# Opening of a transformer-block kernel: running sum of squares moved from GpSimd to VectorE, and two tiles of v ahead of the sums

## The chip, the cores and the metric

One Trainium2 chip, one of its cores. The metric is the device time of one execution in microseconds (us); lower is better. Times of a kernel are medians over several executions. In the text PE is TensorE (matrix multiply), DVE is VectorE, ACT is ScalarE, POOL is GpSimd, SP is the engine that only issues transfers here.

## The reference, cut to what matters

The kernel computes one residual block over L = 1040 positions (16 meta tokens and 1024 frames) of width 1024, in float32. What the change touches is the first normalisation and the projections that follow it:

```python
def _rmsnorm(x, w):
    x32 = x.astype(jnp.float32)
    y = x32 * lax.rsqrt(jnp.mean(x32 * x32, axis=-1, keepdims=True) + EPS)
    return (y * w.astype(jnp.float32)).astype(x.dtype)
...
    n1 = _rmsnorm(h, norm1_w)
    proj = n1 @ w_in.astype(h.dtype)
    q, k, v, fg, u = jnp.split(
        proj, [D_ATTN, 2 * D_ATTN, 3 * D_ATTN, 3 * D_ATTN + N_HEADS], axis=-1)
    q = _rmsnorm(q.reshape(B, L, N_HEADS, HEAD_DIM), q_norm_w).transpose(0, 2, 1, 3)
    k = _rmsnorm(k.reshape(B, L, N_HEADS, HEAD_DIM), k_norm_w).transpose(0, 2, 1, 3)
```

Forgetting attention over 8 heads, pooling heads, an output projection and a SwiGLU feed-forward part come after it and are not touched.

## The kernel before, in words

**Layout.** The input arrives transposed, as hT: 8 tiles (`KT`) of 128 rows of the width by 1040 positions. Since the factor rsqrt(mean) belongs to a position, it can be multiplied in after the projection; the projections therefore start on x times the norm's weight while the sums of squares are still being made.

**Split products.** Each matrix product runs as three products of rounded operands: high by high, low by high, high by low. A tile is split by ACT writing the rounded high part (`xh`, L187; `wh`, L157 and L125) and DVE writing the rest (`xl`, L188; `wl`, L160 and L128). For the weights of v DVE also writes the last 384 columns of the high part (L159).

**The opening loop (L175 to L218), one pass for each of the 8 row tiles k.** SP loads xs (L179, L181). ACT writes xh (L187), DVE writes xl (L188). ACT squares xs into a tile of its own (L197 for k = 0, which is the accumulator `sqacc`, L200 for the others), and POOL adds that tile to `sqacc` (L201). PE multiplies: the first pair of heads of k (`k0_ps`, 3 PSUM banks) and the forget gate (`fg_ps`, 3 banks) take 9 matmuls that need xh alone (L205 to L207) and then 6 that need xl (L209, L210), 15 in all for each k. At k = 3 seven small loads are issued from ACT's queue (L213, L216). At k = 6 and 7 `prep_v` loads and splits the first two of the four weight pairs of v; the other two follow behind the loop (L223). The raw weights pass through three staging buffers (`aux`), which they share with the weight `wk0s` and the later projections, so the fourth raw pair is loaded into the buffer of the first, once DVE's split of the first (L160) is done.

**Behind the loop.** ACT takes the gate's sums out of PSUM (L227). `v_mm(j)` makes the tile of v for 128 positions, 24 matmuls of 512 columns into one bank (L240 to L242), and `v_evac(j)` takes it out, scaled by the norm's factor (L247), which is why it must wait for that factor. Before the change `v_mm(0)` comes first; then `sqacc` is split (L125 by ACT, L128 by DVE), PE sums it over the partitions, once into a column form (`pc`, 18 small matmuls, L258, L259) and once into a row form (three banks, L271, L272), and DVE and ACT make the factor `rcol` from `pc` (L264 to L268) and the row `qrow` (L273). Then come `v_mm(1)`, the normalisation of the first heads of k (`qk_evac`, matmuls L287, L288), and the loop of the other seven tiles of v (L378), into which the steps of the generator `gates()` (L318) are placed at j = 2, 4, 6 and 8.

**What sets the order.** The kernel runs under a manual schedule: each engine's instructions stand in the order in which the code writes them, and an instruction waits in it for whatever made its inputs and for the last reader of a buffer that it overwrites. PSUM has 8 banks here, handed out in the order in which they came free (`PSP`, L50). ACT, SP and POOL each have one queue, in program order, for computing and for issuing transfers alike.

```python
            sq = ut(L, FT, "sq")
            A.activation(sq, xs, AF.Square)
            G.tensor_tensor(sqacc, sqacc, sq, op=OP.add)
```

Of the kernel before, what the change touches and what calls it, by code (L numbers as in the profile page):

```python
# [7 lines left out]
FT = mybir.dt.float32  # L8
FR = mybir.dt.float32r
AF = mybir.ActivationFunctionType  # L10
OP = mybir.AluOpType
# [3 lines left out]
KT = D // 128  # L15
META = 16
SEQ = 1024
L = META + SEQ
# [5 lines left out]
ST = 9  # L24
# [3 lines left out]
CHQ = ((16, 512), (528, 512))  # L28
PRE = 1
VC, VK = 640, 6  # L30
RA, LW = 10, 4
NB = (3, 6)
CW, KW, SW, W1 = 2, 2, 3, 3
# [12 lines left out]
def block_kernel(ctx, tc, hT, n1w, w_f, w_v, w_u, w_qk, b_f, qnw, knw, w_pool, pscale, w_out, n2w, w_g, w_up, w_d, outT):  # L46
# [8 lines left out]
    def nm(s):  # L55
        cnt[0] += 1
        return f"{s}_{cnt[0]}"

    def ut(cols, dt=FT, s="u"):
        return U.tile([128, cols], dt, tag="u", bufs=NU, padded_shape=None, name=nm(s))  # L60
# [4 lines left out]
    def ps(s="ps"):  # L65
        return PSP.tile([128, 512], FT, tag="ps", name=nm(s))

    def const(shape, dt, s):
        return U.tile(shape, dt, name=s, bufs=1)

    def f(ap):
        return ap.bitcast(FT)

    mm = nc.tensor.matmul
    V, A, G = nc.vector, nc.scalar, nc.gpsimd

    def table(i):

        A.add_instruction(mybir.InstLoadActFuncSet(name=nc.get_next_instruction_name(), engine=mybir.EngineType.Activation,
                                                   act_func_set_id=i, ins=[], outs=[]))  # L80
# [41 lines left out]
    def split_w(stage, cols, mk, he, le):  # L122
        h, l = mk(cols, FR, "wh"), mk(cols, FR, "wl")
        if he is A:
            A.activation(h, stage, AF.Copy)  # L125
        else:
            he.tensor_copy(h, stage)
        le.tensor_tensor(l, stage, f(h), op=OP.subtract)  # L128
        return h, l

    def load(src, cols, mk, eng=None):
        t = mk(cols, FT, "wst")
        (eng or nc.sync).dma_start(t, src)
        return t
# [4 lines left out]
    def rsqrt_newton(g, t, tmp, e1=None):  # L139

        (e1 or V).tensor_tensor(tmp, t, g, op=OP.mult)
        V.scalar_tensor_tensor(tmp, tmp, -0.5, g, op0=OP.mult, op1=OP.mult)
        V.scalar_tensor_tensor(g, tmp, 1.5, g, op0=OP.add, op1=OP.mult)


    table(6)
    xh, xl = [], []
    sqacc = None
    wfs = const([128, KT, 16], FR, "wfs")
    fg_ps = [ps("fg") for _ in CH3]  # L150
    k0_ps = [ps("k0") for _ in CH3]
# [2 lines left out]
    def prep_v(i):  # L154
        s = load(w_v[:, 2 * i:2 * i + 2, :].rearrange("p k f -> p (k f)"), 1024, aux)
        h, l = ut(1024, FR, "wh"), ut(1024, FR, "wl")
        A.activation(h[:, :VC], s[:, :VC], AF.Copy)  # L157
        if VC < 1024:
            V.tensor_copy(h[:, VC:], s[:, VC:])  # L159
        V.tensor_tensor(l, s, f(h), op=OP.subtract)  # L160
        wv.append((h, l))
# [5 lines left out]
    def wk0_split(W):  # L167
        A.activation(wk0h[:, W], wk0s[:, W], AF.Copy)
        V.tensor_tensor(wk0l[:, W], wk0s[:, W], f(wk0h)[:, W], op=OP.subtract)
# [5 lines left out]
    for k in range(KT):  # L175
        xs = ut(L, FT, "xs")
        if k == 0:
            for o, n in CH3:
                nc.sync.dma_start(xs[:, o:o + n], hT[:, 0, o:o + n])  # L179
        else:  # L180
            nc.sync.dma_start(xs, hT[:, k, :])  # L181
        if k == 0:
            wk0_split(slice(0, 128))
            wf3 = wf.rearrange("p (k f) -> p k f", k=KT)
        h, l = ut(L, FR, "xh"), ut(L, FR, "xl")
        for o, n in CH3 if k == 0 else [(0, L)]:
            A.activation(h[:, o:o + n], xs[:, o:o + n], AF.Copy, scale=n1[:, k:k + 1])  # L187
            V.scalar_tensor_tensor(l[:, o:o + n], xs[:, o:o + n], n1[:, k:k + 1], f(h)[:, o:o + n], op0=OP.mult, op1=OP.subtract)  # L188
            if k == 0 and o == 0:
                V.tensor_copy(wfs[:, :, 0:8], wf3)  # L190
                V.tensor_tensor(wfs[:, :, 8:16], wf3, f(wfs)[:, :, 0:8], op=OP.subtract)
        xh.append(h)
        xl.append(l)
        if k == 0:
            wk0_split(slice(128, 1024))
            sqacc = ut(L, FT, "sqacc")
            A.activation(sqacc, xs, AF.Square)  # L197
        else:
            sq = ut(L, FT, "sq")
            A.activation(sq, xs, AF.Square)  # L200
            G.tensor_tensor(sqacc, sqacc, sq, op=OP.add)  # L201
        s0, s1 = k == 0, k == KT - 1
        W = slice(128 * k, 128 * k + 128)
        for c, (o, n) in enumerate(CH3):
            mm(k0_ps[c][:, :n], wk0h[:, W], h[:, o:o + n], start=s0, stop=False)  # L205
            mm(k0_ps[c][:, :n], wk0l[:, W], h[:, o:o + n], start=False, stop=False)
            mm(fg_ps[c][:16, :n], wfs[:, k, :], h[:, o:o + n], start=s0, stop=False)  # L207
        for c, (o, n) in enumerate(CH3):
            mm(k0_ps[c][:, :n], wk0h[:, W], l[:, o:o + n], start=False, stop=s1)  # L209
            mm(fg_ps[c][:16, :n], wfs[:, k, :], l[:, o:o + n], start=False, stop=s1)  # L210
        if k == 3:
            for t, src in ((n2, n2w), (psc, pscale), (bfg, bass.AP(tensor=b_f.tensor, offset=b_f.offset, ap=[[0, 128], [1, NH]]))):
                A.dma_start(t, src)  # L213
            for t, src in ((qw, qnw), (kw, knw)):
                for i in range(2):
                    A.dma_start(t[64 * i:64 * i + 64], src)  # L216
        if k >= VK:
            prep_v(k - VK)  # L218
# [3 lines left out]

    for i in range(KT - VK, 4):  # L223
        prep_v(i)
    fgT = ut(L, FT, "fgT")
    for c, (o, n) in enumerate(CH3):
        A.activation(fgT[:16, o:o + n], fg_ps[c][:16, :n], AF.Copy)  # L227
# [5 lines left out]
    def v_mm(j):  # L233
        sz = min(128, L - 128 * j)
        T = slice(128 * j, 128 * j + sz)
        p = ps("v")
        for k in range(KT):
            vh, vl = wv[k // 2]
            W = slice(512 * (k % 2), 512 * (k % 2) + 512)
            mm(p[:sz], xh[k][:, T], vh[:, W], start=k == 0, stop=False)  # L240
            mm(p[:sz], xh[k][:, T], vl[:, W], start=False, stop=False)  # L241
            mm(p[:sz], xl[k][:, T], vh[:, W], start=False, stop=k == KT - 1)  # L242
        return p

    def v_evac(j, p):
        sz = min(128, L - 128 * j)
        A.activation(v32[j // 2][:sz, 512 * (j % 2):512 * (j % 2) + 512], p[:sz], AF.Copy, scale=rcol[:sz, j:j + 1])  # L247

    vp = v_mm(0)


    acch, accl = split_w(sqacc, L, ut, A, V)
# [26 lines left out]
    def qk_evac(p, n, cols, w, out):  # L279
        h, l, s = hs(n, FR, "sqh"), hs(n, FR, "sql"), hs(n, FT, "sq")  # L280
        A.activation(h, p[:, :n], AF.Square)
        A.activation(s, p[:, :n], AF.Square)
        V.tensor_tensor(l, s, f(h), op=OP.subtract)

        def rest():
            p2 = ps("ss")
            mm(p2[:, :n], bones, h, start=True, stop=False)  # L287
            mm(p2[:, :n], bones, l, start=False, stop=True)  # L288
            t, g, s2 = hs(n, FT, "t"), hs(n, FT, "g"), hs(n, FT, "s2")
            V.scalar_tensor_tensor(t, qrow[:, cols], 64.0 * EPS, p2[:, :n], op0=OP.mult, op1=OP.add)  # L290
            A.activation(g, t, AF.Ln)
            A.activation(g, g, AF.Exp, scale=-0.5)  # L292
            G.tensor_tensor(s2, t, g, op=OP.mult)  # L293

            def last():
                V.scalar_tensor_tensor(s2, s2, -0.5, g, op0=OP.mult, op1=OP.mult)
                V.scalar_tensor_tensor(g, s2, 1.5, g, op0=OP.add, op1=OP.mult)
                V.scalar_tensor_tensor(out, p[:, :n], w, g, op0=OP.mult, op1=OP.mult)
            later.append(last)
        later.append(rest)  # L300
# [5 lines left out]
    k32[0] = ut(L, FT, "k32")  # L306
    for (o, n), p in zip(CH3, k0_ps):
        qk_evac(p, n, slice(o, o + n), kw, k32[0][:, o:o + n])
    vn = v_mm(1)
    v_evac(0, vp)  # L310
    vp = vn
    now, later[:] = later[:], []
    run_later(now)
# [59 lines left out]
    def load_w(x):  # L373
        c, i = order[x]
        return load((w_u[i] if c == "u" else w_qk[2 * i + (c == "k")]).rearrange("p k f -> p (k f)"), 1024, aux)

    gt = gates()
    for j in range(2, ST):  # L378
        vn = v_mm(j)
        v_evac(j - 1, vp)  # L380
        vp = vn
        if j % 2 == 0:
            next(gt, None)
        if j == 2:
            A.activation(rb, qrow, AF.Ln)
            A.activation(rb, rb, AF.Exp, scale=-0.5)
            rtm = ut(L, FT, "rtm")
            rsqrt_newton(rb, qrow, rtm)
        if j == 6:
            staged.append(load_w(0))  # L390
        if j == 7:
            staged.append(load_w(1))
            wcur = split_w(staged.pop(0), 1024, ut, A, V)
# [1050 lines left out]
```

## Time and profile before

| | |
|---|---|
| median of 3 executions | 1170.41 us (1169.87 to 1171.07) |
| the profiled execution, its own time | 1168.22 us |
| its span in the profile | 1166.4 us |
| its mean granted clock of PE | 0.99 |
| PE busy | 1122.6 us (96%) |
| DVE busy | 764.6 us (66%) |
| ACT busy | 487.1 us (42%) |
| POOL busy | 405.7 us (35%) |

All rows below come from the one profiled execution; its own time is 1.8 us over its span and 2.2 us under the median. Times in rows are microseconds from the start of the span. In a timeline a row gives the start, the length, the engine, the line of the kernel, the operation, what it writes <- what it reads with shapes, the count of merged instructions, and in brackets how long the engine had been idle and what ended that. The length of a merged row runs from the first start to the last end. Engines with a q (ACTq, SPq) are the queues that issue transfers. A PE row's length includes its drain, which overlaps the next matmul, so PE's pace is read from the differences of starts. A granted clock of 1.00 is 2.4 GHz, 0.50 is 1.2 GHz; a value between is a mean over both.

### The profile page before, as it was taken

To read this page: it belongs to the slowest core of one execution; us is meant where nothing else is said; L and a number is where in the kernel's file an instruction comes from. 1 tells how busy PE (TensorE), PEld (TensorE's weight loads), DVE (VectorE), ACT (ScalarE), POOL (GpSimd) and SP (SyncE) were. 2 spreads that over 40 slices of the span, in tenths; PEclk is the share of its full clock that TensorE was granted. 3 is DMA by queue.
4 is the path that set the end of the run, shared out by engine and by line. 5 is a ranking of instruction groups with operands and counts; after the bars stand their busy time and mean duration, and the time that the engine had idled before them with its cause. 6 is when DMAs were issued, how large, how long until landed. Compare 5 with 4: busy or idle time off the path is not lost.

```text
span 1166.4 us, 14589 instructions
## 1 busy us (share of the span) xinstructions
PE 1122.6 (96%) x5251; PEld 920.6 (79%) x5251; DVE 764.6 (66%) x1230; ACT 487.1 (42%) x907; POOL 405.7 (35%) x336
## 2 busy tenths in 40 slices
PE   6899999999999999998999999999999999999997
PEld 5787999887878888676888888888888888888874
DVE  7524763675778886899554455455544588698775
ACT  7333431541778776543422233223322345353432
POOL 6200235241445565638454335433543310000000
PEclk9899999999999999998999999999999999999999
DMA  6201110251012113320322122212221577632552
GB/s 220 73 1 51 40 55 10 64 164 46 20 31 47 29 42 115 117 99 1 109 91 90 56 89 90 91 52 93 90 91 55 190 285 294 198 135 91 174 185 83
DMA packets 48407, 112.45 MB, mean 96 GB/s; under 512 B 6560, under 2 KB 9120, under 8 KB 48336
## 3 DMA queue, kind: packets, MB, share of 16 engines
q1 hardware_dynamic: 38512, 95.23, 25.2%
q10 hardware_dynamic: 9824, 16.30, 3.7%
q8 instruction: 41, 0.67, 0.2%
q14 instruction: 30, 0.25, 0.1%
HBM read 86.10 MB, written 19.92 MB: 91 GB/s over the span
## 4 chain that ended last, share of the span: by engine, by line
PE 80%; DVE 13%; ACT 4%; issue 2%; DMA 0%; ACTq 0%; POOL 0%; SPq 0%; DVEq 0%; POOLq 0%
PE gu L1114 11%; PE gu L1115 11%; PE gu L1113 11%; PE d L1358 5%; PE d L1356 5%; PE d L1357 5%; PE pj L402 3%; PE pj L401 3%; PE pj L403 3%; PE o L500 2%; PE o L501 2%; PE o L502 2%; PE v L240 2%; PE v L242 1%; PE v L241 1%
## 5 line engine op out<-in xcount | busy, mean ns | idle before, releaser
L1114 PE MATMUL gu<-cb,ws 128*128 128x512 f32 x560 | 221.6, 396 | 4.1 <-DVE ws L1104 4.1
L1115 PE MATMUL gu<-cb,ws 128*128 128x512 f32 x560 | 221.6, 396 | 0.0
L1113 PE MATMUL gu<-cb,ws 128*128 128x512 f32 x560 | 221.0, 395 | 0.0
L1104 DVE TENSOR_TENSOR ws<-wst,ws 128x512 fp32r<-128x512 f32 x120 | 98.3, 819 | 124.8 <-ACT ws L1103 124.8
L1114 PEld LDWEIGHTS gu<-cb,ws 128*128 128x128 f32 x560 | 105.7, 189 | 29.6 <-DVE ws L1104 4.5
L1103 ACT ACTIVATE ws<-wst 128x512 fp32r<-128x512 f32 x120 | 70.0, 622 | 138.3 <-POOL wst L1098 130.2
L1356 PE MATMUL d<-hd,wd 128*128 128x512 f32 x308 | 121.7, 395 | 5.8 <-ACT hd L1046 5.8
L1113 PEld LDWEIGHTS gu<-cb,ws 128*128 128x128 f32 x560 | 105.7, 189 | 24.7
L1115 PEld LDWEIGHTS gu<-cb,ws 128*128 128x128 f32 x560 | 105.8, 189 | 24.6
L1358 PE MATMUL d<-hd,wd 128*128 128x512 f32 x308 | 121.9, 396 | 0.4
L1357 PE MATMUL d<-hd,wd 128*128 128x512 f32 x308 | 121.1, 393 | 0.0
L1127 POOL TENSOR_TENSOR e<-e,e 128x512 f32<-128x512 f32 x20 | 29.6, 1479 | 158.4 <-DVE e L1140 105.4
L736 POOL TENSOR_TENSOR pl<-p,ph 128x512 fp32r<-128x512 f32 (+4 forms) x58 | 64.2, 1120 | 44.8 <-ACT p L728 42.8
L1356 PEld LDWEIGHTS d<-hd,wd 128*128 128x128 f32 x308 | 57.9, 188 | 20.7 <-ACT hd L1046 7.8
L402 PE MATMUL pj<-xh,wl 128*128 128x346 f32 (+2 forms) x216 | 72.9, 338 | 0.0
L401 PE MATMUL pj<-xh,wh 128*128 128x346 f32 (+2 forms) x216 | 72.9, 337 | 0.0
L403 PE MATMUL pj<-xl,wh 128*128 128x346 f32 (+2 forms) x216 | 72.9, 337 | 0.0
L1358 PEld LDWEIGHTS d<-hd,wd 128*128 128x128 f32 x308 | 57.9, 188 | 15.6 <-DVE hd L1047 2.5
L1357 PEld LDWEIGHTS d<-hd,wd 128*128 128x128 f32 x308 | 57.9, 188 | 13.3
L293 POOL TENSOR_TENSOR s<-t,g 128x346 f32<-128x346 f32 (+2 forms) x20 | 21.5, 1082 | 131.8 <-ACT g L292 124.7
L1046 ACT ACTIVATE hd<-wst 128x512 fp32r<-128x512 f32 x77 | 48.0, 623 | 21.4 <-DVE wst L1023 16.2
L1047 DVE TENSOR_TENSOR hd<-wst,hd 128x512 fp32r<-128x512 f32 x77 | 52.9, 687 | 4.1 <-ACT hd L1046 4.1
(290 smaller groups left out, 2554.9 us busy)
## 6 DMA issues: line engine op xcount, KB each, us to landing
wst<-in_w_d SPq DMA_DIRECT2D x77, 256.0 KB, 3.3
wst<-in_w_g SPq DMA_DIRECT2D x22, 512.0 KB, 5.2
wst<-in_w_up SPq DMA_DIRECT2D x22, 512.0 KB, 3.5
wst<-hidd SPq DMA_DIRECT2D x22, 512.0 KB, 7.4
wst<-in_w_d SPq DMA_DIRECT2D x11, 512.0 KB, 4.6
hidd<-e ACTq DMA_DIRECT2D x20, 256.0 KB
h<-in_hT SPq DMA_DIRECT2D x8, 512.0 KB, 8.4
h2d<-h SPq DMA_DIRECT2D x16, 256.0 KB, 2.0
```

The costliest lines, as they stand in the source:

```text
L401: mm(p[:, :n], wh[:, W], xh[k][:, o:o + n], start=k == 0, stop=False)
L402: mm(p[:, :n], wl[:, W], xh[k][:, o:o + n], start=False, stop=False)
L403: mm(p[:, :n], wh[:, W], xl[k][:, o:o + n], start=False, stop=k == KT - 1)
L736: sub.tensor_tensor(pl[:sz, o0:o1], p32[:sz, o0:o1], f(ph)[:sz, o0:o1], op=OP.subtract)
L1103: A.activation(t[:, :512], src, AF.Copy)
L1104: E.tensor_tensor(t[:, 512:], src, f(t)[:, :512], op=OP.subtract)
L1113: mm(p, w[:, W], c[:, :512], start=k == 0, stop=False)
L1114: mm(p, w[:, Wl], c[:, :512], start=False, stop=False)
L1115: mm(p, w[:, W], c[:, 512:], start=False, stop=k == 3)
L1356: mm(p, w[:, W], h[:, LO], start=i == 0, stop=False)
L1357: mm(p, w[:, Wl], h[:, LO], start=False, stop=False)
L1358: mm(p, w[:, W], h[:, HI], start=False, stop=i == NPR - 1)
```

## The change

The squares are no longer written to tiles of their own: `square(k)` squares the loaded tile in place, one pass later (at k it squares tile k - 1, tile 7 behind the last `prep_v`). The adds move from POOL to DVE (`sq_add`) and add tiles 1 to 7 into tile 0: three of them in the loop, behind xl of k = 3, 4 and 5, and four behind the last weight split of v. POOL's seven adds are gone. `v_mm(1)` moves ahead of the sums over the partitions, `v_mm(2)` takes its old place, both first tiles are taken out behind it, and the loop over the rest starts at j = 3, with the first step of `gates()` at j = 3 and the others, as before, at 4, 6 and 8.

```diff
--- before.py
+++ after.py
@@ -28,6 +28,7 @@
 CHQ = ((16, 512), (528, 512))
 PRE = 1
 VC, VK = 640, 6
+SQ = 4
 RA, LW = 10, 4
 NB = (3, 6)
 CW, KW, SW, W1 = 2, 2, 3, 3
@@ -144,8 +145,15 @@
 
 
     table(6)
-    xh, xl = [], []
-    sqacc = None
+    xh, xl, sqs = [], [], []
+
+    def square(k):
+
+        A.activation(sqs[k], sqs[k], AF.Square)
+
+    def sq_add(k):
+        V.tensor_tensor(sqs[0], sqs[0], sqs[k], op=OP.add)
+
     wfs = const([128, KT, 16], FR, "wfs")
     fg_ps = [ps("fg") for _ in CH3]
     k0_ps = [ps("k0") for _ in CH3]
@@ -191,14 +199,13 @@
                 V.tensor_tensor(wfs[:, :, 8:16], wf3, f(wfs)[:, :, 0:8], op=OP.subtract)
         xh.append(h)
         xl.append(l)
+        sqs.append(xs)
         if k == 0:
             wk0_split(slice(128, 1024))
-            sqacc = ut(L, FT, "sqacc")
-            A.activation(sqacc, xs, AF.Square)
         else:
-            sq = ut(L, FT, "sq")
-            A.activation(sq, xs, AF.Square)
-            G.tensor_tensor(sqacc, sqacc, sq, op=OP.add)
+            square(k - 1)
+        if k >= 3 and k - 2 < SQ:
+            sq_add(k - 2)
         s0, s1 = k == 0, k == KT - 1
         W = slice(128 * k, 128 * k + 128)
         for c, (o, n) in enumerate(CH3):
@@ -222,6 +229,10 @@
 
     for i in range(KT - VK, 4):
         prep_v(i)
+    square(KT - 1)
+    for k in range(SQ, KT):
+        sq_add(k)
+    sqacc = sqs[0]
     fgT = ut(L, FT, "fgT")
     for c, (o, n) in enumerate(CH3):
         A.activation(fgT[:16, o:o + n], fg_ps[c][:16, :n], AF.Copy)
@@ -246,7 +257,7 @@
         sz = min(128, L - 128 * j)
         A.activation(v32[j // 2][:sz, 512 * (j % 2):512 * (j % 2) + 512], p[:sz], AF.Copy, scale=rcol[:sz, j:j + 1])
 
-    vp = v_mm(0)
+    v0, vp = v_mm(0), v_mm(1)
 
 
     acch, accl = split_w(sqacc, L, ut, A, V)
@@ -306,8 +317,9 @@
     k32[0] = ut(L, FT, "k32")
     for (o, n), p in zip(CH3, k0_ps):
         qk_evac(p, n, slice(o, o + n), kw, k32[0][:, o:o + n])
-    vn = v_mm(1)
-    v_evac(0, vp)
+    vn = v_mm(2)
+    v_evac(0, v0)
+    v_evac(1, vp)
     vp = vn
     now, later[:] = later[:], []
     run_later(now)
@@ -375,13 +387,13 @@
         return load((w_u[i] if c == "u" else w_qk[2 * i + (c == "k")]).rearrange("p k f -> p (k f)"), 1024, aux)
 
     gt = gates()
-    for j in range(2, ST):
+    for j in range(3, ST):
         vn = v_mm(j)
         v_evac(j - 1, vp)
         vp = vn
-        if j % 2 == 0:
+        if j == 3 or j % 2 == 0:
             next(gt, None)
-        if j == 2:
+        if j == 3:
             A.activation(rb, qrow, AF.Ln)
             A.activation(rb, rb, AF.Exp, scale=-0.5)
             rtm = ut(L, FT, "rtm")
```

## Rows read from the trace of the kernel before

**Rows 1.** The page, part 4: the chain that ended last, its shares by engine.

```profile
PE 80%; DVE 13%; ACT 4%; issue 2%; DMA 0%; ACTq 0%; POOL 0%; SPq 0%; DVEq 0%; POOLq 0%
```

**Rows 2.** Windows: us, busy time (instructions) of PE, PEld, DVE, ACT, POOL; clock, DMA share, GB/s.

```profile
15.00:30.00 15.00, 11.98 (x69) 8.97 (x70) 15.00 (x5) 10.12 (x12) 14.69 (x5) 1.00 0.52 199
30.00:45.00 15.00, 10.64 (x42) 8.30 (x40) 11.26 (x12) 2.72 (x5) 3.18 (x2) 0.77 0.43 140
```

**Rows 3.** Waits of PE: line, who was waited for, us in total, times, longest.

```profile
PE k L209 <- DVE xl L188: 7.8, 6, 4.4
```

**Rows 4.** Line 201 on POOL: ns of one add, least, median, most; first and last start.

```profile
L201 POOL TENSOR_TENSOR sqacc<-sqacc,sq x7: 2380/3312/3329, 11.2 to 30.9; 128x1040 f32<-128x1040 f32 x7
```

**Rows 5.** Timeline of DVE in the opening.

```profile
10.22 1.30 DVE L188 SCALAR_TENSOR_TENSOR xl<-xs,n,xh 128x1040 fp32r<-128x1040 f32 x1 [0.92 <-ACT xh L187]
12.24 16.29 DVE L188 SCALAR_TENSOR_TENSOR xl<-xs,n,xh 128x1040 fp32r<-128x1040 f32 x5 [0.72 <-ACT xh L187]
...
34.26 1.29 DVE L188 SCALAR_TENSOR_TENSOR xl<-xs,n,xh 128x1040 fp32r<-128x1040 f32 x1
...
37.13 0.35 DVE L159 CAST wh<-wst 128x384 fp32r<-128x384 f32 x1
...
38.73 0.35 DVE L159 CAST wh<-wst 128x384 fp32r<-128x384 f32 x1
...
40.92 1.24 DVE L128 TENSOR_TENSOR wl<-sqacc,wh 128x1040 fp32r<-128x1040 f32 x1 [0.51 <-ACT wh L125]
...
47.90 1.36 DVE L273 TENSOR_SCALAR qrow<-ps 128x348 f32<-128x348 f32 x3
...
68.47 1.24 DVE L141 TENSOR_TENSOR rtm<-qrow,rb 128x1040 f32<-128x1040 f32 x1 [3.19 <-ACT rb L386]
69.74 1.24 DVE L142 SCALAR_TENSOR_TENSOR rtm<-rtm,rb 128x1040 f32<-128x1040 f32 x1
```

**Rows 6.** Timeline of PE in the opening, single matmuls that begin a group of them.

```profile
10.58 0.32 PE L205 MATMUL k<-xh,wh 128*128 128x348 f32 x1
...
12.95 0.32 PE L205 MATMUL k<-xh,wh 128*128 128x348 f32 x1
...
14.98 0.42 PE L209 MATMUL k<-xl,wh 128*128 128x348 f32 x1 [0.47 <-DVE xl L188]
...
35.60 0.66 PE L209 MATMUL k<-xl,wh 128*128 128x348 f32 x1 [4.36 <-DVE xl L188]
...
37.50 0.63 PE L240 MATMUL v<-wh,xh 128*128 128x512 f32 x1
...
44.74 0.16 PE L258 MATMUL ps<-ones,wh 128*128 128x2 f32 x1
...
47.53 0.40 PE L240 MATMUL v<-wh,xh 128*128 128x512 f32 x1
...
53.12 0.32 PE L287 MATMUL ss<-sqh,bones 128*128 128x348 f32 x1
```

**Rows 7.** Timeline of ACT and of its queue in the opening.

```profile
8.07 1.05 ACT L197 ACTIVATE sqacc<-xs 128x1040 f32<-128x1040 f32 x1
9.03 1.15 ACT L187 ACTIVATE xh<-xs,n 128x1040 fp32r<-128x1040 f32 x1
...
10.66 0.33 ACTq L213 DMA_DIRECT2D n<-in_n2w  x1
...
11.05 1.15 ACT L187 ACTIVATE xh<-xs,n 128x1040 fp32r<-128x1040 f32 x1
...
14.33 0.62 ACTq L216 DMA_DIRECT2D kw<-in_knw  x1
...
21.13 0.72 ACT L157 ACTIVATE wh<-wst 128x640 fp32r<-128x640 f32 x1
...
38.17 0.74 ACT L157 ACTIVATE wh<-wst 128x640 fp32r<-128x640 f32 x1 [13.05 <-DMA wst<-in_w_v]
```

**Rows 8.** Timeline of SP's queue: the load of the fourth weight pair of v.

```profile
34.36 0.33 SPq L133 DMA_DIRECT2D wst<-in_w_v  x1
```

## The prediction

> **What bounds the kernel now.** I read the page's chain first: PE holds 80% of the chain that ended last [rows 1], so time is won only where PE stands still or runs slowly. Next, the windows: from 15 to 30 us PE is busy for 11.98 of 15 us, DVE for all 15.00 and POOL for 14.69; from 30 to 45 us PE is busy for 10.64 us and its granted clock falls to 0.77 [rows 2]. Then PE's waits: six times it waits for DVE's xl, 7.8 us in all, 4.4 us at the longest [rows 3]. DVE's timeline tells why it is late. xl of k = 1 takes 1.30 us and that of k = 7 takes 1.29 us; between them five take 16.29 us, 3.26 each [rows 5]. POOL's seven adds run from 11.2 us, each 2.38 us at least and 3.31 at the median [rows 4], so exactly where both engines work, each of their instructions takes longer. The change takes POOL out of this stretch and has nothing else of POOL's there.
>
> PE's own rows give the price. A pass of 15 matmuls that waits for nothing takes 2.37 us, from 10.58 to 12.95. Passes 1 to 7 would take 7 x 2.37 = 16.6 us, but they last until 37.50, which is 26.9 us. The first tile of v then takes 7.24 us (37.50 to 44.74) and the second 5.59 us (47.53 to 53.12): the first began at the lower of the two clock levels, after the 4.36 us of idling at 35.60. Sums stand between them, 2.79 us [rows 6]. So what the contention costs PE is 10.3 us of waiting and restarting and 1.65 us of slow clock, 12.0 together. PE's idle gaps of 0.47 us and the like from 14.98 on [rows 6] left the clock at 1.00 [rows 2], so short gaps after the change should too.
>
> **The change part by part.** All times are on the clock of the profiled execution (1168.22 us, span 1166.4, so 1.8 us lie around it; the median, 1170.41, is 2.2 higher).
>
> *Adds on DVE.* Seven adds of 1040 columns, no such row, but the nearest is DVE's split of sqacc, same shape and two operands in SBUF: 1.24 us, and dependent ones follow each other at 1.27 us (68.47 to 69.74) [rows 5]. 7 x 1.27 = 8.9 us of DVE, against at least 5 x (3.26 - 1.30) = 9.8 us that its xl get back. Bounds: 1.24 and, if something still disturbs them, POOL's undisturbed 2.38 [rows 4]; I take 1.27, an engine's own row.
>
> *Adds off POOL.* Seven instructions go, 3.31 us each at the median [rows 4]. ACT's rounding of the sum waits for DVE's last add from now on, not for POOL's.
>
> *Squares in place, one pass later.* ACT does as many instructions, but a square now overwrites what DVE's xl reads, so it waits for DVE. What is queued behind it matters: the seven small loads on ACT's queue stand behind `square(2)`. In the old kernel they go out from 10.66 us while xh of k = 2 starts only at 11.05, ahead of the engine, and take until 14.33 + 0.62 = 14.95, 4.29 us [rows 7]. Afterwards xh of k = 1 can start where the first square did, 8.07, and k = 2 follows a pitch of 2.02 later (9.03 to 11.05), at 10.09 [rows 7]; its xl is done at 10.09 + 1.15 + 1.34 = 12.6. If the queue holds the loads back until then, they end at 16.9 and xh of k = 4 starts there instead of at 15.1. No row shows ACT's queue held by DVE; SP's load of the fourth v pair leaves at 34.36, as DVE goes on to its next instruction at 34.26 [rows 5, 8], which is a queue held so. Bounds: 0 and 2.0 us of delay; I take 2.0. SP's queue keeps its order, and its loads that wait for these small ones come up to 2 us later, still ahead of their use.
>
> *The passes afterwards.* PE wants xh of k = 4 at 10.58 + 3 x 2.37 = 17.7 and has it at 16.95 + 1.15 = 18.1: 0.4 us idle. From there ACT goes on at 2.02 a pass, plus 0.62 for the first weight pair (21.13 is followed by the next 0.62 later), and xh of k = 7 is done at 24.8. DVE: xl 4 to 19.4, add to 20.7, xl 5 to 22.0, add to 23.2, xl 6 to 24.5, the first weight pair (1.60 us from one pair to the next, 37.13 to 38.73 [rows 5]) to 26.1, xl 7 to 27.3. PE wants xl 6 at 24.3 and xl 7 at 26.9: some 0.7 us idle with restarts. The passes end at 28.3, not 37.5.
>
> *Weights of v.* The fourth raw pair is issued when the first pair's split frees its buffer: 26.1, not 34.36. ACT got it 3.81 us after the issue (34.36 to 38.17 [rows 7, 8]): 29.9. DVE ends its split at 32.2; PE, at 5.59 / 24 = 0.233 a matmul, wants it 18 matmuls into the first tile, 28.3 + 4.2 = 32.5. No wait, with 0.3 us to spare.
>
> *Two tiles of v ahead.* Four adds follow the splits, 32.2 + 4 x 1.27 = 37.3; ACT's rounding and DVE's rest take 1.1 and 1.24, so the split sum is there at 39.65. PE ends both tiles at 28.3 + 2 x 5.59 = 39.5. Cost 0.15 us; had only one tile stood ahead, PE would have waited 5.7 us here. So the two tiles are the cover of the adds, and each further us on DVE's chain now costs PE nearly one.
>
> *PSUM.* With two tiles held, k's three banks and three more make eight. The column sums and the row sums need four, so one of the row sums takes the column sums' bank again, and `v_mm(2)` must wait until DVE has taken out the first row sum. That ends at about 47.90 + 1.36 / 3 = 48.4 on the old clock, PE being free at 47.53 [rows 5, 6]: 0.9 us that were not there. Bounds: 0 (a bank free in time) and 1.7 (the third taken out); I take 0.9.
>
> *Later steps.* The first gate step moves behind `v_mm(3)`, and one tile of v, 5.6 us of PE, still hides its chain on DVE and ACT ahead of the second step; without that cover it would cost up to those 5.6 us. I cost it at nothing.
>
> Sum: 39.65 + 2.79 + 0.9 = 43.3 where the old kernel has done the same work at 53.12 [rows 6]. Gain 9.8 us: 1170.4 - 9.8 = 1160.6.
>
> A rule that speaks against this change: the Trainium skill, Perfetto Trace Analysis, section Optimizing Scalar/DVE Operations, says that if VectorE is saturated, it may make sense to move work off it, to GpSimd even. By it the sum would be that of the last rival, 1175.1, against 1160.6 by the rows.
>
> **The rivals.** *The queue does not hold* (0 instead of 2.0 us). Then PE never waits in the loop and ends it at 27.2; DVE's sum is there at 37.7, ahead of PE's 38.35; with 2.79 and 0.9 it is 42.0, a gain of 11.1: 1159.3. For it: nothing shows ACT held by DVE. Against: program order.
>
> *The fourth pair comes late.* Its load now has a weight load behind it sooner, and ran alone before. If it takes twice 3.8 us, PE idles 3.5 us in the first tile and 0.4 before the sums: gain 5.9, 1164.5; half of that gives 1162.5. A raw x tile later than 8.07 (the second is seen used only at 9.03 [rows 7]) would cost up to 1 us in the same way.
>
> *Given back later.* PE reaches a stage that is paced by loads, and waits there: 1170.4. Against: the chain has 0% DMA [rows 1].
>
> *Slower: DVE is simply full.* If xl is slow because ACT and the loads write at the same time, not because of POOL, it keeps its pace, and three adds lengthen the passes to 37.50 + 3 x 1.27 = 41.3. Then 7.24 + 5.59 for v at the old clock, 2.79 and 0.9 give 57.8 against 53.12: 4.7 us slower, 1175.1. It decides as long as xl gets back less than those 4.7 us of its 9.8. For it: 15.00 of 15 us [rows 2]. Against: xl of k = 1, at 1.30 us [rows 5], runs while ACT writes xh and squares [rows 7] and before POOL's first add at 11.2 [rows 4].
>
> The rule of the Trainium skill's page Perfetto Trace Analysis, section Optimizing Scalar/DVE Operations, would make this of the change; by the two short xl the trace bears it out little.
>
> That the change doesn't do what it says is hardly possible: POOL has no other work in the stretch.
>
> **How the numbers follow.** As summed 0.55; queue does not hold 0.15; fourth pair or raw tile late 0.20; given back 0.05; slower 0.05. The range reaches from the second case with no bank wait, 1158.4, less 0.6 us for the spread of the runs, to the third at its dearest: 1157.8 to 1164.6. It leaves out the last two cases and their like. About 0.2%, 2.3 us, is what a measurement of this kernel can tell from no change; the first three cases are all faster by more: 0.90, within 0.05, slower 0.05.
>
> **What would show it.** Right: xl at 1.3 us for all k; PE's wait for xl under 1.5 us in all, a short one for xh of k = 4; the passes ending near 28 and the granted clock at 1.00 from 15 to 45; DVE's last add near 37; a wait of `v_mm(2)` for L273 of about 0.9 us; from there on the same work some 9.8 us earlier to the end. The small loads going out at 12.6 show the held queue, at 10.7 the other case. Wrong: xl still at 3 us with POOL idle, or PE standing still before the sums for more than 1 us, or a later wait that was not there.

## The result, and the profile after

| | before | after |
|---|---|---|
| median beside each other | 1170.74 us (4 runs, 1169.87 to 1172.73) | 1161.59 us (4 runs, 1160.71 to 1162.16) |
| profiled execution, its span | 1168.22, 1166.4 us | 1162.12, 1160.0 us |

The ratio is 0.9919, with a 95% interval of 0.9902 to 0.9936: 9.2 us less, where 9.8 were forecast. A second measurement (e5, below) gave 0.9914 (0.9893 to 0.9936).

The changed kernel's lines are numbered up to 12 higher. The windows that answer to [rows 2], with 60 to 75 us added (columns as there):

```profile
15.00:30.00 15.00, 15.00 (x94) 12.48 (x93) 12.77 (x15) 10.55 (x12) 0.00 (x0) 1.00 0.70 223
30.00:45.00 15.00, 14.22 (x70) 11.71 (x69) 11.03 (x20) 6.83 (x16) 0.00 (x0) 0.93 0.30 102
...
60.00:75.00 15.00, 15.00 (x62) 12.12 (x61) 6.39 (x18) 7.31 (x10) 0.00 (x0) 0.89 0.00 0
```

From 15 to 30 us PE is busy all the time and POOL never. DVE, which has three of the seven adds to do there as well, is less busy than before: 12.77 us. DVE's groups by line from 9 to 45 us (busy, then mean ns of one, after the count):

```profile
L196 DVE SCALAR_TENSOR_TENSOR xl<-xs,n,xh 128x1040 fp32r<-128x1040 f32 x7 | 9.1, 1298 | 3.8 <-ACT xh L195 3.8
L155 DVE TENSOR_TENSOR xs<-xs,xs 128x1040 f32<-128x1040 f32 x7 | 8.7, 1238 | 0.2
```

All seven xl take 1.30 us, which answers to the 16.29 us for five in [rows 5]; the adds take 1.24. From the list of PE's waits over the whole span, the new one:

```profile
PE v L251 <- DVE qrow L284: 0.8, 1, 0.8
```

The 7.8 us for xl [rows 3] are gone from the list; what is left of the opening is the start, 6.2 us for the first xh, some short waits that stood there before, and a new wait of 0.8 us for L284, the PSUM bank. PE's timeline, answering to [rows 6]: the first matmuls of passes 1 and 2, of the first tile of v and of the sums:

```profile
10.88 0.49 PE L212 MATMUL k<-xh,wh 128*128 128x348 f32 x1
...
13.88 0.32 PE L212 MATMUL k<-xh,wh 128*128 128x348 f32 x1
...
28.13 0.39 PE L251 MATMUL v<-wh,xh 128*128 128x512 f32 x1
...
39.23 0.17 PE L269 MATMUL ps<-ones,wh 128*128 128x2 f32 x1
```

From 13.88 us on a pass takes 2.37 us and nothing stands between the passes; the first tile begins at 28.13, not 37.50, and at full pace. Then the third tile (`v_mm(2)`), the matmuls behind it, and the gate's:

```profile
43.09 0.80 PE L251 MATMUL v<-wh,xh 128*128 128x512 f32 x1 [0.78 <-DVE qrow L284]
...
50.27 0.32 PE L298 MATMUL ss<-sqh,bones 128*128 128x348 f32 x1
...
56.89 2.08 PE L334 MATMUL z<-sel,fgT 16*128 16x8 f32 x18
```

The third tile begins at 43.09 us. The kernel before had this much work done at 53.12 [rows 6], so 10.0 us are won here. But this tile takes 7.18 us (43.09 to 50.27), not 5.59: 1.6 us are lost to the clock, which is 0.50 from 44 to 46 us. A second fall follows behind the gate's small matmuls at 56.89, and the window from 60 to 75 us has 0.89. They are 3.2 of the 3.6 us by which the two profiled spans differ less (6.4 us) than the starts of the third tile: the profiled execution of before had a clock of 1.00 in both places, and at 1168.22 it was faster than every run in its row of the table.

ACT and its queue, the one load on SP's queue, and DVE's last adds with the split behind them, answering to [rows 7], [rows 8] and [rows 5]:

```profile
13.12 0.33 ACTq L220 DMA_DIRECT2D n<-in_n2w  x1
...
15.66 1.26 ACTq L223 DMA_DIRECT2D kw<-in_knw  x2
16.97 1.16 ACT L195 ACTIVATE xh<-xs,n 128x1040 fp32r<-128x1040 f32 x1 [2.24 <-DMA qw<-in_qnw]
...
29.61 0.74 ACT L165 ACTIVATE wh<-wst 128x640 fp32r<-128x640 f32 x1 [2.03 <-DMA wst<-in_w_v]
```

```profile
25.83 0.33 SPq L134 DMA_DIRECT2D wst<-in_w_v  x1
```

```profile
31.79 5.14 DVE L155 TENSOR_TENSOR xs<-xs,xs 128x1040 f32<-128x1040 f32 x4
38.07 1.24 DVE L129 TENSOR_TENSOR wl<-xs,wh 128x1040 fp32r<-128x1040 f32 x1 [1.14 <-ACT wh L126]
```

The small loads leave from 13.12 us (10.66 before) to 15.66 + 1.26 = 16.92, and xh of k = 4 starts behind them at 16.97. The fourth raw pair of v is issued at 25.83 instead of 34.36. The last add ends at 36.9, the split sum is there at 39.3; PE, at 39.23, does not wait.

### The profile page after: what moved, and what is told of

The parts are those of the page before. It is cut to its first block, busy times and chain, and to the rows that moved or that the text cites. A ratio compares the mean times of both kernels' runs of the same rounds, so it can differ in the third digit from the quotient of the medians.

```text
span 1160.0 us, 14579 instructions
## 1 busy us (share of the span) xinstructions
PE 1121.8 (97%) x5251; PEld 921.7 (79%) x5251; DVE 759.7 (65%) x1237; ACT 486.5 (42%) x907; POOL 384.0 (33%) x329
## 4 chain that ended last, share of the span: by engine, by line
PE 82%; DVE 13%; ACT 3%; issue 2%; DMA 0%; POOL 0%; SPq 0%; ACTq 0%; DVEq 0%; POOLq 0%
PE gu L1126 11%; PE gu L1127 11%; PE gu L1125 11%; PE d L1370 5%; PE d L1368 5%; PE d L1369 5%; PE pj L413 3%; PE pj L414 3%; PE pj L415 3%; PE o L512 2%; PE o L513 2%; PE o L514 2%; PE v L251 2%; PE v L253 2%; PE v L252 2%
```

## The experiments

Three theories were set against each other. **Contention:** POOL's adds and DVE's instructions hold each other up; taking POOL out frees the passes, and the second tile of v covers the adds that are left. **Order:** most of the gain is the place of the second tile. **Full DVE:** xl was slow because ACT and the loads write at the same time. The kernels e1 to e4 shared 29 runs of the kernel before (median 1169.52 us), e5 to e8 shared 11 on another chip (median 1171.31).

### e1: POOL busy again, and nobody waits for it

```diff
             square(k - 1)
+            if k == 1:
+                junk = ut(L, FT, "junk")
+            G.tensor_tensor(junk, f(h) if k == 1 else junk, f(h), op=OP.add)
```

> The changed kernel, and in the loop POOL adds xh of k = 1 to 7 into a tile that nothing reads (7 adds of 1040 columns, where it added squares before; the output does not depend on them). Theory (POOL and DVE hold each other up): DVE's xl of 1040 columns takes about 3.3 us again and so do DVE's own adds in the loop, 7 x about 2 us more on DVE; the passes end at 38 to 41 us instead of 28.1, the time is 1172 to 1177 us. Rival (xl was slow because ACT and the loads write at the same time): nobody waits for these adds, so xl stays at 1.30 us and the time at 1161.6 us.

Measured: 1171.42 us, ratio to before 1.0020 (1.0007 to 1.0033). The whole gain is gone, though no instruction depends on the added ones. DVE's timeline and POOL's in this kernel:

```profile
9.36 1.30 DVE L196 SCALAR_TENSOR_TENSOR xl<-xs,n,xh 128x1040 fp32r<-128x1040 f32 x1
...
23.58 3.46 DVE L155 TENSOR_TENSOR xs<-xs,xs 128x1040 f32<-128x1040 f32 x1
26.96 3.41 DVE L196 SCALAR_TENSOR_TENSOR xl<-xs,n,xh 128x1040 fp32r<-128x1040 f32 x1
30.30 1.23 DVE L155 TENSOR_TENSOR xs<-xs,xs 128x1040 f32<-128x1040 f32 x1
31.45 1.29 DVE L196 SCALAR_TENSOR_TENSOR xl<-xs,n,xh 128x1040 fp32r<-128x1040 f32 x1
...
34.26 3.46 DVE L196 SCALAR_TENSOR_TENSOR xl<-xs,n,xh 128x1040 fp32r<-128x1040 f32 x1
```

```profile
12.51 16.76 POOL L209 TENSOR_TENSOR junk<-junk,xh 128x1040 f32<-128x1040 f32 x5
33.30 3.31 POOL L209 TENSOR_TENSOR junk<-junk,xh 128x1040 f32<-128x1040 f32 x1 [4.02 <-ACT xh L195]
```

Adds and xl of DVE take 3.4 us while POOL adds. Then comes a control within the run: POOL has finished its fifth merged add at 12.51 + 16.76 = 29.3 us and waits for the next xh until 33.30. DVE's add at 30.30 and its xl at 31.45 fall into this gap and take 1.23 and 1.29 us, with ACT at work (2.29 of the 2.40 us from 30.3 to 32.7). The xl at 34.26 meets POOL's last add and takes 3.46. The loads rest in that gap (0.04 of the DMA engines' time), so the opposite case is needed too, and the window from 26 to 29 us has it (columns as in [rows 2]):

```profile
26.00:29.00 3.00, 1.70 (x6) 0.92 (x5) 3.00 (x2) 0.00 (x0) 2.99 (x1) 0.66 0.00 0
```

ACT and the DMA engines do nothing here, POOL adds, and the xl at 26.96 takes 3.41 us. In the changed kernel, the other way round, the xl from 18.17 us takes 1.30 with ACT busy throughout and the DMA engines busy for 0.94 of the time (18.2 to 19.4). Full DVE is out; contention is shown. The last pass ended near 39 us, as expected; the time came out 0.6 us under the range given.

The Trainium skill, GPSIMD Engine Reference, section Key points, says that GpSimd shares its memory interfaces with VectorE and contends with VectorE's instructions that have two SBUF inputs. By that rule these rows are what one expects, and the trace agrees: 1.30 us alone, 3.4 beside POOL.

### e2 and e3: each half of the change alone

e2 keeps the adds on DVE and has one tile of v ahead of the sums, as before:

```diff
-    v0, vp = v_mm(0), v_mm(1)
+    vp = v_mm(0)
...
-    vn = v_mm(2)
-    v_evac(0, v0)
-    v_evac(1, vp)
+    vn = v_mm(1)
+    v_evac(0, vp)
...
-    for j in range(3, ST):
+    for j in range(2, ST):
```

> The changed kernel with only one tile of v ahead of the sums, v_mm(1) behind them as before. Theory (the second tile is the cover of the adds): PE is through the first tile at 33.7 us and the split sum is there at 38.0 to 39.3 us, so PE waits 4.3 to 5.5 us; a low clock behind that costs up to 1.7 us, the wait for a PSUM bank (0.8 us) goes: 1165 to 1168 us. Rival (most of the gain is the order of the v tiles): 1169 us or more.

Measured: 1168.34 us, ratio 0.9989 (0.9977 to 1.0001). PE's timeline, the first two matmuls of the sums and the first behind the next tile of v:

```profile
37.76 0.37 PE L269 MATMUL ps<-ones,wh 128*128 128x2 f32 x1 [3.93 <-ACT wh L126]
39.03 0.37 PE L270 MATMUL ps<-ones,wl 128*128 128x2 f32 x1 [0.90 <-DVE qcol L273]
...
50.81 0.32 PE L298 MATMUL ss<-sqh,bones 128*128 128x348 f32 x1
```

PE stands still for 3.93 us before the sums and 0.90 behind their first matmul, as the theory had it (4.3 to 5.5 in all), but what follows cost more than forecast: with the idling came the low clock (0.50 from 40 to 46 us), and the sums and the tile behind them last from 37.76 to 50.81, 13.1 us, where 2.8 + 5.6 would do. The time lies 0.3 us over the range given.

e3 is the kernel before with the other half, the order of the tiles (e2's diff the other way round).

> The kernel before with the order of the v tiles alone changed (two ahead of the sums); squares in their own tiles and adds on POOL as before. Theory: xl still takes 3.3 us, the passes end at 37.5 us, POOL's sum is ready early anyway, so the second tile covers nothing and the PSUM bank adds its wait of 0.8 us: 1170.7 to 1172.5 us. Rival (most of the gain is the order): 1165 us or less.

Measured: 1170.51 us, ratio 1.0018 (1.0002 to 1.0034), no gain and a trace of loss; the time lies 0.2 us under the range given, the kernel before having a median of 1169.52 beside it. DVE's five xl, and PE's third tile with the matmul behind it:

```profile
12.18 16.28 DVE L188 SCALAR_TENSOR_TENSOR xl<-xs,n,xh 128x1040 fp32r<-128x1040 f32 x5 [0.71 <-ACT xh L187]
```

```profile
53.01 0.80 PE L240 MATMUL v<-wh,xh 128*128 128x512 f32 x1 [0.78 <-DVE qrow L273]
...
60.05 0.32 PE L287 MATMUL ss<-sqh,bones 128*128 128x348 f32 x1
```

xl is as slow as in [rows 5], so the second tile covers nothing, and the wait for the bank is there, 0.78 us, with a slow tile behind it (7.0 us). Order alone is out. **Neither half gives much: adds moved 0.1% less (not told from none), order 0.2% more, both 0.8% less.** Moving the adds ends the passes 9.4 us sooner; without a tile to compute meanwhile, PE waits out half of that and pays with its clock.

### e4, e5, e6: the wait for the PSUM bank and the clock

e4 and e6 are the same kernel; DVE takes the row sums out ahead of the chain that makes rcol:

```diff
+    for c, (o, n) in enumerate(CH3):
+        p = ps()
...
+        V.tensor_scalar(qrow[:, o:o + n], p[:, :n], 1.0 / D, EPS, op0=OP.mult, op1=OP.add)
     A.activation(rcol, qcol, AF.Ln)
     A.activation(rcol, rcol, AF.Exp, scale=-0.5)
     rsqrt_newton(rcol, qcol, rtmp)
-    for c, (o, n) in enumerate(CH3):
-        p = ps()
...
-        V.tensor_scalar(qrow[:, o:o + n], p[:, :n], 1.0 / D, EPS, op0=OP.mult, op1=OP.add)
```

> The changed kernel with the row sums over the partitions taken out by DVE ahead of the chain that makes rcol, so that v_mm(2) has its PSUM bank when PE is free. Theory: PE's wait of 0.78 us for L284 goes; if the low clock in v_mm(2) (7.2 us instead of 5.6) hangs on that wait, it goes too: 1159.2 to 1160.8 us. Rival (the clock falls because of the 18 small matmuls of the sums, whatever stands behind them): v_mm(2) still takes about 7.2 us and only 0.8 us is gained, 1160.8 us; at the other end, the wait was hidden and nothing is gained, 1161.6 us.

Measured: 1159.73 us, ratio 0.9915 (0.9898 to 0.9932). First matmul of the third tile and first behind it in e4:

```profile
42.13 0.50 PE L251 MATMUL v<-wh,xh 128*128 128x512 f32 x1
...
47.79 0.32 PE L298 MATMUL ss<-sqh,bones 128*128 128x348 f32 x1
```

The wait is gone and the tile takes 5.7 us (42.13 to 47.79); every window from 30 to 90 us has a clock of 1.00. Its time can't be set against 1161.59, which was measured beside slower runs of the kernel before. For a verdict on time e5, the changed kernel unaltered, and e6 ran side by side:

> The changed kernel unaltered, beside the others on one chip. Theory: a gain of 9 us on before, a wait of 0.8 us of PE for L284, and behind it v_mm(2) at the lower clock, 7.0 to 7.2 us, as in the first profile. Rival (the low clock there was chance): v_mm(2) takes 5.6 us.

> The kernel of e4_rowsums_first a second time, beside the changed kernel on one chip. Theory (the wait for the bank brings the low clock): no wait, v_mm(2) in 5.6 us at a clock of 1.00, and 1.5 to 2.5 us less than the changed kernel. Rival (chance of one profile): v_mm(2) is slow here too, and the gain on the changed kernel is 0.8 us or less.

Measured: e5 1161.88 us, ratio 0.9914 (0.9893 to 0.9936); e6 1160.63 us, 0.9910 (0.9890 to 0.9931). The wait is worth 1.3 us by the medians, short of the 1.5 to 2.5 expected; the intervals overlap, so in time no gain is shown, only in the rows. e5's third tile and the matmul behind it:

```profile
42.81 0.51 PE L251 MATMUL v<-wh,xh 128*128 128x512 f32 x1 [0.78 <-DVE qrow L284]
...
50.05 0.32 PE L298 MATMUL ss<-sqh,bones 128*128 128x348 f32 x1
```

It takes 7.24 us again. So the tile behind the wait was slow in the first profile, in e3, here and in e9 (below, 8.2 us); without the wait it was fast in e4, e6 and e8. But e1 and e7 (below) have the wait and a fast tile (5.7 us each). And in e9 the clock fell first: it is 0.60 from 45.5 to 46.0 us, while the row sums still run, and 0.50 from 46.0 to 46.8, and the wait ends at 46.80:

```profile
46.80 0.79 PE L259 MATMUL v<-wh,xh 128*128 128x512 f32 x1 [0.55 <-DVE qrow L292]
```

So the low clock goes with the wait in four profiles of six, but the wait need not be its cause. The rival written down for e4, the 18 small matmuls of the sums, is not out; what brings the low clock here stays open. And e6 loses elsewhere: its clock is 0.93 from 45 to 60 us and 0.96 from 60 to 75, where e4, the same kernel, has 1.00. Falls behind the gate's small matmuls (L334, which end at 56.5 us in e6) come in some executions and not in others; that these matmuls bring them was not tried.

### e7 and e8: squares in tiles of their own

```diff
     def square(k):
-        A.activation(sqs[k], sqs[k], AF.Square)
+        sq = ut(L, FT, "sq")
+        A.activation(sq, sqs[k], AF.Square)
+        sqs[k] = sq
```

> The changed kernel with the squares in tiles of their own again, so that a square waits for nothing on DVE. Theory (ACT's queue is held by the square's wait for xl, but PE has time): the small loads go out at about 10.7 to 11.2 us instead of 13.1, xh of k = 4 starts near 15 us instead of 16.97, and the passes still end at about 28 us: the time of the changed kernel within 0.5 us. Rival (the held queue costs what the prediction summed): 1.3 us faster than the changed kernel.

Measured: 1159.52 us, ratio 0.9897 (0.9875 to 0.9919), 2.4 us under e5 by the medians, again with overlapping intervals. ACT and its queue in e7, then PE's passes 1 and 4 and the first tile of v, in e7 and in e5 (there with pass 7 too):

```profile
11.04 0.33 ACTq L222 DMA_DIRECT2D n<-in_n2w  x1
...
15.11 1.17 ACT L197 ACTIVATE xh<-xs,n 128x1040 fp32r<-128x1040 f32 x1 [0.49 <-issue]
```

```profile
10.12 0.32 PE L214 MATMUL k<-xh,wh 128*128 128x348 f32 x1
...
17.22 0.32 PE L214 MATMUL k<-xh,wh 128*128 128x348 f32 x1
...
26.70 0.39 PE L253 MATMUL v<-wh,xh 128*128 128x512 f32 x1
```

```profile
10.01 0.32 PE L212 MATMUL k<-xh,wh 128*128 128x348 f32 x1
...
17.84 0.42 PE L212 MATMUL k<-xh,wh 128*128 128x348 f32 x1 [0.58 <-ACT xh L195]
...
25.46 0.43 PE L212 MATMUL k<-xh,wh 128*128 128x348 f32 x1 [0.20 <-ACT xh L195]
...
27.96 0.40 PE L251 MATMUL v<-wh,xh 128*128 128x512 f32 x1
```

The loads leave at 11.04 us and xh of k = 4 starts at 15.11, as expected. But by the rows the theory written down for this run fell and its rival held. In the first profile of the change PE began pass 1 late (10.88) and slowly, a matmul each 0.29 us and from 12.30 on each 0.16, so xh of k = 4 came in time. (The profile gives a granted clock of 1.00 from the first microsecond on, so this slow start can't be read from that column.) In e5 pass 1 begins at 10.01; PE then waits 0.58 us for xh in pass 4 and 0.20 in pass 7, and ends its passes at 27.96. In e7 pass 1 begins at 10.12 and the passes end at 26.70, 1.3 us sooner. The held queue sets a floor near 28 us under the passes, and whether PE touches it hangs on how early PE comes to its full pace. e7's third tile, behind the same wait for a bank, for the count above:

```profile
41.56 0.50 PE L253 MATMUL v<-wh,xh 128*128 128x512 f32 x1 [0.77 <-DVE qrow L286]
...
47.22 0.32 PE L300 MATMUL ss<-sqh,bones 128*128 128x348 f32 x1
```

e8 has both edits.

> Row sums first and squares in tiles of their own, together. Theory: as e6_rowsums_again, within 0.5 us. Rival (the held queue costs): 1.3 us faster than e6_rowsums_again.

Measured: 1156.98 us (four runs, 1156.89 to 1157.67), ratio 0.9877 (0.9852 to 0.9902). This is the fastest kernel of the study, 14.3 us under before and 4.9 under the unaltered change, whose runs beside it (1158.54 to 1164.99) lie above all of its own. The window of e8 in which the clock of e6 fell:

```profile
45.00:60.00 15.00, 15.00 (x76) 12.42 (x76) 2.64 (x10) 6.37 (x11) 2.74 (x3) 1.00 0.00 1
```

The clock is 1.00 here and in the windows beside it, so it does not fall up to 75 us. Against e6 it gains 3.7 us, more than either forecast. Its passes end 0.75 us sooner (27.18 against 27.93), and its first projection matmul starts 2.35 us sooner (84.75 against 87.10); the difference of 1.6 us goes with the clock, which fell in e6's profiled execution and not here. The last 1.3 us come later in the kernel and were not followed up. Why e8's runs agree so closely was not tried.

### e9: which work of POOL hurts

```diff
             square(k - 1)
+            if k == 1:
+                junk, junk2 = ut(L, FT, "junk"), ut(L, FT, "junk2")
+            if k < 4:
+                G.tensor_copy(junk, f(h))
+            else:
+                G.tensor_copy(junk[:, 0:8], f(h)[:, 0:8])
+                for _ in range(3):
+                    G.memset(junk2, 0.0)
```

> The changed kernel with POOL work that nothing reads, of two kinds: at k = 1 to 3 POOL copies xh (one operand, 1040 columns), at k = 4 to 7 it fills a tile with zeros three times (no operand, 1040 columns each) behind a copy of 8 columns. Theory (what hurts is POOL reading or writing beside a DVE instruction with two operands in SBUF, whatever POOL does): xl of k = 1 to 3 takes about 1.3 us plus the time of the copy, and xl and adds of k = 4 to 7 are stretched by the fills too. Rival (only POOL's two-operand adds hurt): all xl stay at 1.30 us. Between them (reads hurt, writes don't): xl 1 to 3 long, xl 4 to 7 at 1.30 us.

Measured: a single run, 1168.57 us, taken for the durations alone. POOL's first and third copy and the xl beside each; then DVE at k = 6 and three fills of POOL:

```profile
9.51 1.05 POOL L210 COPY junk<-xh 128x1040 f32<-128x1040 f32 x1 [6.04 <-ACT xh L195]
...
13.95 2.12 POOL L210 COPY junk<-xh 128x1040 f32<-128x1040 f32 x1 [1.29 <-ACT xh L195]
```

```profile
9.48 2.17 DVE L196 SCALAR_TENSOR_TENSOR xl<-xs,n,xh 128x1040 fp32r<-128x1040 f32 x1
...
13.85 1.30 DVE L196 SCALAR_TENSOR_TENSOR xl<-xs,n,xh 128x1040 fp32r<-128x1040 f32 x1
```

```profile
23.88 3.12 POOL L214 MEMSET junk<- 128x1040 f32 x3
```

```profile
23.81 1.30 DVE L196 SCALAR_TENSOR_TENSOR xl<-xs,n,xh 128x1040 fp32r<-128x1040 f32 x1
25.02 1.07 DVE L167 CAST wh<-wst 128x384 fp32r<-128x384 f32 x1
26.20 1.22 DVE L168 TENSOR_TENSOR wl<-wst,wh 128x1024 fp32r<-128x1024 f32 x1
```

Beside the first copy, 1.05 us, xl takes 2.17 instead of 1.30, and so does the next. Beside fills, xl takes 1.30 (at 23.81, with fills from 23.88 to 27.00), and the split at 26.20, which begins while a fill runs, takes 1.22, as without fills (1.23 in the changed kernel). So an instruction with two operands suffers from POOL's reading, not from its writing: the middle answer. It needs one limit: at k = 3 the xl that begins 0.10 us ahead of the third copy keeps its 1.30 us, the copy is stretched to 2.12, and DVE's add behind that xl, begun while the copy runs, takes 2.09. In e1 it is the same with the xl at 9.36, 1.30 us, and POOL's first add from 9.40. So of an overlapping pair one instruction is held, and not always DVE's. The cast of 384 columns, 0.35 us alone [rows 5], takes 1.07 beside the fills, although it has one operand.

## Why the prediction was right, point by point

- **What bounds the kernel.** Right: xl at 1.30 us for all k, the passes ending at 28.13 (28.3 forecast), the gain at the start of the third tile 10.0 us (9.8). e1 shows the cause by itself.
- **Adds on DVE.** 1.24 us each, the last ending at 36.9 (37.3). That the adds need the second tile as cover is shown by e2; the 5.7 us of waiting given for it were 4.8, and a low clock came on top, which cost more than 3 us.
- **The held queue.** Chosen without a row for it, and right: the loads leave at 13.12 (12.6), xh of k = 4 starts at 16.97 (16.95). PE's idling of 1.1 us did not show in the first profile, because pass 1 began 0.3 us later than assumed and took 3.0 us instead of 2.37; in e5 against e7 it is there, 1.3 us. That the passes ended within 0.2 us of the forecast in the first profile was luck: the two errors cancelled.
- **The fourth pair.** Used 3.78 us after its issue (3.81), the split done at 31.9 (32.2); no wait.
- **The PSUM bank.** 0.78 us (0.9); with DVE's row sums moved forward (e4, e6) it is gone.
- **What was mis-sized.** "Short gaps after the change should" leave the clock alone. They did in the passes, as in [rows 2], but not behind the sums: the third tile cost 1.6 us more in two profiles of the changed kernel out of two, and of the signs named, a clock of 1.00 from 15 to 45 us did not come (0.93 from 30 to 45). The sum had no term for this. With falls behind the gate's matmuls that come and go it makes the profiled gain 6.4 us where the third tile had 10.0; how much of the 0.6 us between the medians' 9.2 and the forecast it is can't be told without a profile of each execution. e8 has, besides the clock, the held queue and the wait for the bank out of the way.
- **The rivals.** "DVE is simply full" fell with e1. The rule that the prediction quotes against the change from the Trainium skill, Perfetto Trace Analysis, section Optimizing Scalar/DVE Operations, is quoted by half: the next sentence there says that GpSimd and VectorE share an SBUF read port, so that moving work between these two might not help. The rows of e1, 1.23 us for an add in POOL's gap and 3.46 beside its adds, go with that half. "The queue does not hold" fell with the rows of ACT's queue; e7 shows what it would have been worth. No wait for loads gave the gain back later: the first projection matmul starts 6.9 us sooner (89.6 against 96.5), 10.0 less the two falls of the clock, and the last matmul of the down projection's first line 6.4 us sooner (1155.5 against 1161.9), which is 0.5 us less over the whole rest.

## What to carry to other kernels

When DVE is busy for 15 of 15 us, first compare the duration of one of its instructions in and out of the stretch: here the engine was not full, it was held up by another, and taking over that engine's work relieved it. A stretch that is freed needs work to run into, or the next wait takes the gain. And an edit in place adds a wait for the last reader, which holds all that stands behind it in the engine's queue, loads for others included.

## What the runs showed of the hardware that was not expected

- PE's clock fell to the lower level with hardly any idling: in the first profile of the changed kernel behind 18 matmuls of 2 columns and a gap of 0.78 us (a mean of 0.83 over 40 to 50 us), and behind the gate's 18 matmuls of 8 columns with no gap at all (0.83 over 60 to 70 us). Each fall cost about 1.6 us, and the same kernel can have it in one execution and not in another. In e9 it fell before the wait for the bank began, so that gap alone does not explain it.
- POOL's fills leave two-operand instructions of DVE alone and stretch its one-operand cast from 0.35 to 1.07 us; POOL's reads stretch the two-operand ones, or are stretched by them where DVE began first (e9: xl 1.30 and copy 2.12, against 2.17 and 1.05).
- At the start PE's matmuls of 346 columns stand 0.29 us apart and later 0.16, from 9.4 us on in one execution of the changed kernel (e5) and from 12.3 in another, while the granted clock reads 1.00 throughout.
